# Modulation products spread over four column strips of the array, and the residual gate's weights used in fp32 as they are loaded

## The chip, the cores and the metric

The kernel is one program on one core of a Trainium2 chip. Its metric is the device time of a run in microseconds (us). TensorE (PE in the rows; PEld is its weight load) multiplies, VectorE (DVE), ScalarE (ACT) and GpSimd (POOL) do the elementwise work, and the DMA queues that SyncE (SP) and ScalarE issue move data between HBM and the on-chip memories SBUF (inputs of the engines) and PSUM (results of TensorE).

## The reference, cut to what matters

One inference step of a decoder layer with 1024 prompt tokens and 8 decode rows (1032 columns in all), model width 2048, followed by a final norm:

```
mod = silu(c) @ w_ada + b_ada        # c: 9 rows (1 prompt, 8 decode), w_ada: 2048 x 6144
sh, sc, gt = the three thirds of mod
h  = rmsnorm(x) * (1 + sc) + sh
P  = h @ w_in                        # one combined projection
o_s5, o_rw = the two branches, from P
mixed = sigmoid(g_s5) * (o_s5 @ w_out[:1024]) + sigmoid(g_rw) * (o_rw @ w_out[1024:])
x  = x + gt * mixed;   y = rmsnorm(x) * final_g
```

The change concerns only `mod`: its first two thirds (shift and scale), which are needed before `h` and so before everything else, and its last third (the residual gate `gt`), which is needed in the last stage. All tensors are fp32.

## The kernel before

The large products (h @ w_in, the gated linear unit, w_out) run in fp16 halves: weights and data are scaled by a power of two, split into a high and a low half, and three products (high-high, high-low, low-high) are summed. One job is one tile of 128 output channels: 16 row tiles x 3 products x 3 groups of 344 to 347 columns, 144 products of line 436. `weights` prepares the next job's weights beside the running one: `wload` (L354) loads 1 MB on SP's queue into two buffers, `wscale` takes the largest magnitude (DVE L157, then a reduction over partitions on POOL, L154) and `wsplit` makes the halves (ACT L386, DVE L387).

Everything else is written as generators that yield (DVE ns, PE ns, gap ns) per step. The `Driver` books these: each call of `slot` adds the booked PE time to a counter, and a background step is put into the program once the counter has passed its due time (the counter at its last step plus its gap) and the booked DVE time is not more than 0.8 us ahead. `drain` puts in all that is left. This order of the program is only a priority: the planner that lays the instructions on each engine takes, by its own cost model, the first in this order that is ready, so work that stands later can still come earlier on an idle engine. Once laid out, each engine keeps its order and waits.

**Start.** `startup` takes the shift and the scale columns in eight blocks of 512 columns (`mod_block`), scale and shift in turn. A block loads eight slabs of w_ada of 512 KB (L218, SP's queue, four buffers `wa`), and multiplies each in fp32: the 9 columns of silu(c) are the stationary operand and 512 columns of w_ada stream, 16 products in one accumulation on partitions 0 to 8 (L223; each fp32 product shows as two records). Then ACT copies the row out (L225), four transposes put channels on partitions (L229), and DVE adds the biases. In the first four blocks each second slab is followed by a tile of x (`xload`, 516 KB). Beside the blocks run `stats` (sums of squares, the inverse root, x times it: L269 to L284) and `modulate` (L294 to L298), which needs both. The halves of h (L340, L341) come after the last block, and then the first large product.

**Residual gate.** `gt_mod` runs from the end of the recurrence on, beside the gated linear unit and the output jobs. Per tile n of 128 channels it loads 1 MB of w_ada on ACT's queue (L1370, two buffers), no sooner than output job n-2 has begun (`GQ`), takes the largest magnitude of four quarters (DVE L157, POOL L154), splits each into halves (ACT L1393, DVE L1394), and multiplies 32 times with the halves as stationary operand and 18 or 9 streaming columns (L1399, L1400); two DVE steps rescale and add the bias (L1403, L1404). Output job n needs tile n (`need`), and its `final_tiles` scales the loaded gates by it (L1500).

Of the kernel before, what the change touches and what calls it, by code (L numbers as in the profile page):

```python
# [66 lines left out]
class Driver:  # L67
    """Paces background generators against the stream of large products.

    Each generator yields (vector_ns, tensor_ns, gap_ns) per step, or None while  # L70
    something it needs has not been emitted yet.
    """
# [58 lines left out]
class Hybrid:  # L131
# [10 lines left out]
    # ---------------------------------------------------------------- helpers  # L142
    def pow2(self, am, out, n=1):
        """out[:,0,:] = 2^14 / 2^floor(log2 am), out[:,1,:] its inverse, on every partition."""
# [14 lines left out]
    def rsqrt(self, v, y, t):  # L159
        """y = v^-1/2 by ln, exp and one Newton step; t is scratch, v is left as it is."""  # L160
# [7 lines left out]
    def vexp(self, x, k, r, ki):  # L168
        """x = exp(x) on VectorE for small tiles."""
# [15 lines left out]
    # ---------------------------------------------------------------- constants  # L185
# [24 lines left out]
    # ---------------------------------------------------------------- modulation  # L210
    def mod_block(self, col, stage, row, out, xload=None):
        """out(i, psum[128, 9]) for the four 128-channel tiles of modulation columns col..col+511."""
# [3 lines left out]
        for j in range(8):  # L216
            wa = stage(j)
            nc.sync.dma_start(wa, d["w_ada"][256 * j:256 * j + 256, col:col + 512].rearrange("(k p) n -> p k n", p=128))  # L218
            if xload is not None and j % 2:
                xload()  # L220
            for i in range(2):
                kt = 2 * j + i
                nc.tensor.matmul(q[0:9, :], self.csil[:, kt, :], wa[:, i, :], start=(kt == 0), stop=(kt == 15))  # L223
            yield (0, 1716, 0)
        nc.scalar.copy(row, q[0:9, :])  # L225
        yield (0, 0, RGAP)
        q2 = self.ps.tile([128, 4, 16], F32, name="pmt", tag="up")
        for i in range(4):
            nc.tensor.transpose(q2[:, i, 0:9], row[:, 128 * i:128 * i + 128], self.c["ident"][0:9, 0:9])  # L229
        out(q2)  # L230
        yield (300, 1704, 0)

    def startup(self, st, jobs):
        """h = rmsnorm(x) (1 + scale) + shift, as halves under one power of two.

        That power comes from a bound: a normalised row has no element above sqrt(DM).
        """
# [12 lines left out]
        mrow = xp.tile([9, 512], F32, name="mrow")  # L250
# [3 lines left out]
        nc.scalar.activation(out=self.csil, in_=self.csil, func=AF.Silu)  # L254
        H, HL, A = self.H, self.HL, self.As
# [92 lines left out]
    # ---------------------------------------------------------------- large products  # L348
# [8 lines left out]
    def wscale(self, job):  # L357
        """The power of two of a product's weights."""
# [16 lines left out]
    def wsplit(self, job):  # L375
        """Halves of a product's weights."""
# [15 lines left out]
    def weights(self, nxt, after):  # L392
        """Beside a product: the halves of the next one's weights, then the scale of those after them."""
# [14 lines left out]
    def run_jobs(self, jobs):  # L408
        """Runs the products in order; the weights of the next one are split while one runs."""
# [37 lines left out]
    def product_by_rows(self, job):  # L447
        """The first product takes the rows of h as they come."""
# [11 lines left out]
    # ---------------------------------------------------------------- projections  # L460
# [11 lines left out]
    def job_rw(self, idx, dst, flag, need=None, post=None):  # L472
        """A token-shifted tile: dst[:, 0:1032] = p (1 - mu) + p_prev mu."""
# [85 lines left out]
    def job_gate(self, which, n, dst=None):  # L559
        """sigmoid of a gate tile, to scratch in DRAM or to a tile on chip."""  # L560
# [15 lines left out]
    # ---------------------------------------------------------------- RWKV-7  # L576
# [37 lines left out]
    def rw_prep(self):  # L614
        """First half of each pair's preparation: everything that needs no buffer of the running recurrence."""
# [64 lines left out]
    def bdq(self, k):  # L680
        """Block diagonal form of the operands of chunks 2k, 2k+1."""
# [53 lines left out]
    def rw_side(self):  # L735
        """Token-major operands of the recurrence and the bonus term, beside the inversion."""
# [96 lines left out]
    def rw_tail(self):  # L833
        """Group norm, bonus and gate of a pair, beside the operands of the next."""
# [41 lines left out]
    def rw_sample(self):  # L876
        """Operands of the decode rows, with (head parity, pair, row) on partitions."""
# [18 lines left out]
    def sample(self):  # L896
        """One step of the recurrence for the decode rows, where the S5 operand of the outputs will lie."""
# [73 lines left out]
    # ---------------------------------------------------------------- S5  # L971
# [24 lines left out]
    def s5_system(self, st):  # L996
        """Tiles of the discretised system, made beside the modulation."""
# [13 lines left out]
    def il(self, b, g):  # L1011
        """Transposed input operand of group g of block b: it lies where the states of block b + 1 will."""
# [5 lines left out]
    def s5_pre(self):  # L1018
        """Discretised system and its powers; every value lies in both halves of the partitions."""
# [82 lines left out]
    def s5_powers(self, b, name, e1, e2, nt, op):  # L1102
        """[128, 8, nt, 16]: powers of the system on two stacked operands of a block of eight groups."""
# [14 lines left out]
    def s5_outer(self, b):  # L1118
        """Output powers of a block."""
# [5 lines left out]
    def s5_prep(self, b):  # L1125
        """Transposed input powers of a block and the kernel of its chunks."""
# [66 lines left out]
    def s5_runs(self, q):  # L1193
        """States within runs of eight chunks, for a quarter of the groups."""
# [18 lines left out]
    def s5_fix(self, b):  # L1213
        """States before the runs, carried into the chunks of the runs, for a block."""
# [129 lines left out]
    def gt_mod(self, st):  # L1344
# [30 lines left out]
        for n in range(16):  # L1375
# [5 lines left out]
            for q in range(4):  # L1381
                self.absmax(am[:, q:q + 1], w[q], axis=XY)
                yield (600, 0, 0)
# [413 lines left out]
```

## Time and profile before

| what | us |
|---|---|
| median of the 3 runs shown | 3095.9 |
| the runs | 3097.41, 3074.23, 3095.9 |
| span of the profiled execution | 3069.5 |
| TensorE busy in that span | 2792.1 (91%) |
| VectorE busy in that span | 2108.3 (69%) |

The profiled execution's own time is not listed beside its span; the lowest of the three runs lies 4.7 us above the span, the median 26.4 us. In the page's strip of 40 slices of 76.7 us the DMA engines are over 90% busy in the first slice alone, and TensorE is at nine tenths or more in 25 of the 40. The chain of work that ended last is 40% TensorE, 31% VectorE and 16% DMA. All times below are us from the start of the span unless ns is written.

### The profile page before, as it was taken

What the parts mean: (1) busy time and instruction counts of PE and PEld (TensorE: products, weight loads), DVE (VectorE), ACT (ScalarE), POOL (GpSimd) and SP (SyncE); (2) the same over time, 40 slices, a digit from 0 to 9 for tenths busy, and PEclk for the clock granted to TensorE, in tenths of its full rate; (3) what the DMA queues carried; (4) which work ended last, traced back from release to release, by engine and by line L of the source; (5) the groups of instructions that cost most, each with busy time, mean ns of one, the idle gap of its engine ahead of it and who ended that gap; (6) DMA issues with size and microseconds to landing.
All of it is one profiled execution on the core that took longest, in us unless ns stands there. A gap on an engine that the chain in (4) does not pass through costs nothing.

```text
span 3069.5 us, 47775 instructions
## 1 busy us (share of the span) xinstructions
PE 2792.1 (91%) x18266; PEld 1826.5 (60%) x18266; DVE 2108.3 (69%) x5152; ACT 1023.5 (33%) x1783; POOL 472.9 (15%) x764
## 2 busy tenths in 40 slices
PE   7889999999989999899998998999998978888987
PEld 1156666666656666576675665665765645555655
DVE  5589688745675857767668658677675595767765
ACT  2143223425243143242332432432421223433431
POOL 1201000011111111021121110210211122111213
PEclk9999999999999999999999999999999988999999
DMA  9724443331222223213231232132233344843443
GB/s 318 270 63 98 78 92 86 84 95 50 61 66 60 62 55 81 68 45 76 55 81 52 59 80 56 57 75 58 55 82 80 115 154 128 274 121 110 142 124 125
DMA packets 434165, 298.39 MB, mean 97 GB/s; under 512 B 115120, under 2 KB 400464, under 8 KB 432656
## 3 DMA queue, kind: packets, MB, share of 16 engines
q1 hardware_dynamic: 397648, 277.71, 33.1%
q10 hardware_dynamic: 36128, 17.33, 2.0%
q8 instruction: 144, 2.36, 0.3%
q14 instruction: 85, 0.70, 0.1%
q0 software_dynamic: 160, 0.30, 0.0%
HBM read 241.93 MB, written 53.35 MB: 96 GB/s over the span
## 4 chain that ended last, share of the span: by engine, by line
PE 40%; DVE 31%; DMA 16%; issue 6%; ACT 4%; POOL 2%; SPq 1%; ACTq 0%; POOLq 0%; DVEq 0%
PE pg L436 27%; DMA ws<-w_in 5%; DVE TM L781 5%; DMA od<-BV 4%; DVE ZB L783 4%; DVE wlo L387 3%; DVE wam L157 3%; PE pmod L223 2%; DMA ws<-w_out 2%; PE pma L720 2%; PE up L823 1%; PE sp L822 1%; PE up L817 1%; ACT whi L386 1%; DVE OLo L1432 1%
## 5 line engine op out<-in xcount | busy, mean ns | idle before, releaser
L436 PEld LDWEIGHTS <-whi 128*128 128x128 f16 x9600 | 944.8, 99 | 576.7 <-issue 99.8
L436 PE MATMUL pg<-H,whi 128*128 128x344 f16 (+2 forms) x3840 | 1200.7, 313 | 68.6 <-DVE ZB L500 39.1
L436 PE MATMUL pg<-H,wlo 128*128 128x344 f16 (+2 forms) x3840 | 1200.3, 313 | 1.4 <-DVE wlo L387 1.4
L436 PE MATMUL pg<-HL,whi 128*128 128x344 f16 (+2 forms) x3840 | 1200.4, 313 | 0.0
L436 PEld LDWEIGHTS <-wlo 128*128 128x128 f16 x4800 | 475.6, 99 | 256.6 <-issue 17.8
L386 ACT ACTIVATE whi<-ws,wsc 128x512 f16<-128x512 f32 x404 | 265.7, 712 | 489.5 <-DVE wsc L150 315.0
L157 DVE TENSOR_REDUCE wam<-ws 128x1 f32<-128x512 f32 x404 | 266.6, 679 | 137.8 <-DMA ws<-w_in 106.0
L387 DVE SCALAR_TENSOR_TENSOR wlo<-ws,wsc,whi 128x512 f16<-128x512 f32 x404 | 304.3, 780 | 59.3 <-ACT whi L386 58.2
L436 PE MATMUL pg<-OH,whi 128*128 128x344 f16 (+3 forms) x960 | 308.1, 321 | 22.7 <-ACT whi L386 14.9
L436 PE MATMUL pg<-OH,wlo 128*128 128x344 f16 (+3 forms) x960 | 308.0, 321 | 7.8 <-DVE wlo L387 7.8
L436 PE MATMUL pg<-OLo,whi 128*128 128x344 f16 (+3 forms) x960 | 308.3, 321 | 5.0 <-DVE OLo L1432 5.0
L781 DVE TENSOR_TENSOR TM<-ZB 128x252 f32<-128x252 f32 (+52 forms) x504 | 178.7, 355 | 89.1 <-DMA ZB<-c_t 78.6
L783 DVE TENSOR_TENSOR ZB<-ZB,TM 128x252 f32<-128x252 f32 (+52 forms) x504 | 179.8, 357 | 10.5
L154 POOL PARTITION_ALL_REDUCE wg<-wm x105 | 50.6, 482 | 862.0 <-DVE wm L157 452.9
L814 POOL TENSOR_SCALAR SG<-S,GC 128x128 f32<-128x128 f32 x120 | 98.7, 823 | 360.1 <-DVE S L825 224.5
L812 ACT COPY XR<-xp 64x128 f32<-64x128 f32 x128 | 33.0, 258 | 350.2 <-DVE XS L811 334.3
L223 PE MATMUL pmod<-wa,csil 128*9 128x512 f32 x256 | 118.6, 616 | 17.4 <-DMA wa<-w_ada 17.4
L825 DVE SCALAR_TENSOR_TENSOR S<-sp,GC,SG 128x128 f32<-128x128 f32 x120 | 41.6, 347 | 73.0 <-POOL SG L814 37.4
L684 ACT COPY BT<-ZB 64x128 f32<-64x128 f32 x256 | 75.3, 296 | 32.4 <-PE pma L720 23.0
L223 PEld LDWEIGHTS pmod<-wa,csil 128*9 128x9 f32 x256 | 22.3, 93 | 106.1 <-issue 67.0
L817 PE MATMUL up<-XS,TT 128*128 128x128 f32 x256 | 56.7, 304 | 28.1 <-DMA TT<-dT 14.1
L720 PE MATMUL pma<-AR,BT 128*128 128x128 f32 x512 | 71.6, 283 | 4.3 <-DVE AR L711 2.3
(459 smaller groups left out, 3373.4 us busy)
## 6 DMA issues: line engine op xcount, KB each, us to landing
ws<-w_in SPq DMA_DIRECT2D x162, 512.0 KB
wa<-w_ada SPq DMA_DIRECT2D x64, 512.0 KB
sg<-sgd SPq DMA_DIRECT2D x32, 516.0 KB
gw<-w_ada ACTq DMA_DIRECT2D x32, 512.0 KB
ws<-w_out SPq DMA_DIRECT2D x32, 512.0 KB
XT<-xT SPq DMA_DIRECT2D x16, 516.0 KB
xo<-xT SPq DMA_DIRECT2D x16, 516.0 KB
ZB<-dA SPq DMA_DIRECT2D x8, 1024.0 KB
```

What stands on the lines that cost most here:

```text
L154: self.nc.gpsimd.partition_all_reduce(out, in_, 128, bass_isa.ReduceOp.absmax)
L157: self.nc.vector.tensor_reduce(out=out, in_=in_, axis=axis, op=ALU.max, apply_absolute_value=True)
L223: nc.tensor.matmul(q[0:9, :], self.csil[:, kt, :], wa[:, i, :], start=(kt == 0), stop=(kt == 15))
L386: nc.scalar.activation(out=hi[:, ks, :], in_=s, func=AF.Copy, scale=job.sc[:, 0, 0:1])
L387: nc.vector.scalar_tensor_tensor(out=lo[:, ks, :], in0=s, scalar=job.sc[:, 0, 0:1], in1=hi[:, ks, :], op0=ALU.mult, op1=ALU.subtract)
L436: nc.tensor.matmul(q[:, :w], a[:, wk, :], b[:, rk, g0:g1], start=(n == 0), stop=(n == tot - 1))
L684: self.nc.scalar.copy(self.BT[k % 2][i][64 * h:64 * h + 64, :, 64 * h:64 * h + 64], t[64 * h:64 * h + 64, 128 * k:128 * k + 128].rearrange ...
L720: nc.tensor.matmul(q[:, e, 128 * i:128 * i + 128], w[:, e, :], self.AR[:, a, 128 * e:128 * e + 128], start=True, stop=True)
L781: nc.vector.tensor_tensor(out=TM, in0=row.unsqueeze(1).to_broadcast([128, n, m]), in1=TL[:, :n, k:k + 1].to_broadcast([128, n, m]), op=ALU ...
L783: nc.vector.tensor_tensor(out=TL[:, :n, k + 1:], in0=TL[:, :n, k + 1:], in1=TM, op=ALU.subtract)
L814: nc.gpsimd.tensor_scalar(out=self.SG, in0=S0, scalar1=g, scalar2=None, op0=ALU.mult)
L817: nc.tensor.matmul(up[:, 0, :], self.TT[:, a, :], xs, start=True, stop=True)
```

## The change

Both uses of w_ada now go through one helper, `mod_step`. Row tile kt writes its product to the 32 partitions that begin at 32 (kt mod 4), so that four accumulations stand in four column strips of the array. The stationary operand is silu(c) padded with zeros from 9 to 32 columns (`cond`), and the four partial sums are added by one more product with a 0/1 matrix `sel`, which takes the place of the transposes. The residual gate's weights are the streaming operand in fp32, 128 columns at a time; its magnitudes, powers of two, halves and rescaling are gone. The booked times and gaps of the steps change with them. The rest of the diff replaces comment lines by blank ones.

```diff
     def mod_block(self, col, stage, row, out, xload=None):
...
-            for i in range(2):
-                kt = 2 * j + i
-                nc.tensor.matmul(q[0:9, :], self.csil[:, kt, :], wa[:, i, :], start=(kt == 0), stop=(kt == 15))
-            yield (0, 1716, 0)
-        nc.scalar.copy(row, q[0:9, :])
+            self.mod_step(q, self.cs32, wa, 2 * j)
+            yield (0, 600, 0)
+        nc.scalar.copy(row, q)
         yield (0, 0, RGAP)
         q2 = self.ps.tile([128, 4, 16], F32, name="pmt", tag="up")
         for i in range(4):
-            nc.tensor.transpose(q2[:, i, 0:9], row[:, 128 * i:128 * i + 128], self.c["ident"][0:9, 0:9])
+            nc.tensor.matmul(q2[:, i, 0:9], row[:, 128 * i:128 * i + 128], self.sel, start=True, stop=True)
         out(q2)
-        yield (300, 1704, 0)
+        yield (300, 1000, 0)
+
+    def mod_step(self, q, cs, w, k0):
+        for i in range(w.shape[1]):
+            kt = k0 + i
+            s = 32 * (kt % 4)
+            self.nc.tensor.matmul(q[s:s + 32], cs[:, kt, :], w[:, i, :], start=(kt < 4), stop=(kt >= 12))
+
+    def cond(self, pool):
+        t = pool.tile([128, 16, 32], F32, name="cs32", tag="cs32", bufs=1)
+        self.nc.gpsimd.memset(t, 0.0)
+        self.nc.vector.tensor_copy(t[:, :, 0:9], self.csil)
+        self.sel = pool.tile([128, 9], F32, name="sel", tag="sel", bufs=1)
+        w = self.c["ident"].rearrange("p (g x) -> p x g", g=4)[:, 0:9]
+        self.nc.vector.tensor_reduce(out=self.sel, in_=w, axis=AX, op=ALU.add)
+        return t
...
     def startup(self, st, jobs):
-        mrow = xp.tile([9, 512], F32, name="mrow")
+        mrow = t("mrow", 512)
...
+        self.cs32 = self.cond(xp)
...
     def gt_mod(self, st):
-        m, g, cs = small("gcm", 1), small("gcg", 1), small("gcs", 2, 1)
...
+        cs32 = self.cond(pool)
+        yield (300, 0, 2000)
...
             w = load(n)
             yield (0, 0, 6000)
-            am = small("gam", 4, bufs=2)
-            for q in range(4):
-                self.absmax(am[:, q:q + 1], w[q], axis=XY)
-                yield (600, 0, 0)
...
-            self.gmax(g, m1)
-            yield (100, 0, 2500)
-            self.pow2(g, sc)
...
-            for q in range(4):
-                ks = slice(4 * q, 4 * q + 4)
-                nc.scalar.activation(out=hi[:, ks], in_=w[q], func=AF.Copy, scale=sc[:, 0, 0:1])
-                V.scalar_tensor_tensor(out=lo[:, ks], in0=w[q], scalar=sc[:, 0, 0:1], in1=hi[:, ks], op0=ALU.mult, op1=ALU.subtract)
-                yield (700, 0, 0)
-            yield (0, 0, GGAP)
-            q = self.ps.tile([128, 18], F32, name="pmg", tag=("xp", "sp")[n % 2])
-            for k in range(16):
-                nc.tensor.matmul(q, hi[:, k, :], C[:, k, :], start=(k == 0), stop=False)
-                nc.tensor.matmul(q[:, 0:9], lo[:, k, :], C[:, k, 0:9], start=False, stop=(k == 15))
-            yield (0, 1000, 0)
-            gt = self.gt[:, n, :]
-            V.tensor_scalar(out=gt, in0=q[:, 0:9], scalar1=iv, scalar2=c["b_ada"][:, 32 + n:33 + n], op0=ALU.mult, op1=ALU.add)
-            V.scalar_tensor_tensor(out=gt, in0=q[:, 9:18], scalar=iv, in1=gt, op0=ALU.mult, op1=ALU.add)
-            yield (200, 0, 0)
+            q = self.ps.tile([128, 128], F32, name="pmg", tag=("xp", "sp")[n % 2])
+            for h in range(2):
+                self.mod_step(q, cs32, w[h], 8 * h)
+            row = small("grow", 128)
+            nc.scalar.copy(row, q)
+            yield (0, 1300, 1500)
+            q2 = self.ps.tile([128, 16], F32, name="pmh", tag="up")
+            nc.tensor.matmul(q2[:, 0:9], row, self.sel, start=True, stop=True)
+            V.tensor_scalar(out=self.gt[:, n, :], in0=q2[:, 0:9], scalar1=c["b_ada"][:, 32 + n:33 + n], scalar2=None, op0=ALU.add)
+            yield (200, 250, 0)
             self.flags.add(f"gt{n}")
```

## Rows read from the trace of the kernel before

**Rows 1.** The page, part 1: busy us, share of the span, instructions.
```profile
PE 2792.1 (91%) x18266; PEld 1826.5 (60%) x18266; DVE 2108.3 (69%) x5152; ACT 1023.5 (33%) x1783; POOL 472.9 (15%) x764
```
**Rows 2.** DMA totals of 0:150; windows: PE, PEld, DVE, ACT, POOL busy, clock, DMA share, GB/s.
```profile
DMA packets 29243, 45.02 MB, mean 300 GB/s; under 512 B 6018, under 2 KB 10677, under 8 KB 29237
20.00:25.00 5.00, 4.63 (x12) 0.83 (x10) 4.77 (x25) 1.72 (x3) 0.00 (x0) 1.00 1.10 358
50.00:55.00 5.00, 3.76 (x9) 0.91 (x10) 3.71 (x4) 3.31 (x4) 3.03 (x2) 0.66 0.51 193
125.00:130.00 5.00, 5.00 (x13) 1.03 (x12) 5.00 (x6) 0.00 (x0) 4.92 (x2) 1.00 0.87 304
```
**Rows 3.** Chain of waits in the startup: start us, us, what.
```profile
87.52 13.83 PE pmod L223 x32
...
134.33 12.99 PE pmod L223 x30
...
157.29 16.63 DVE HL L341 x14
```
**Rows 4.** PE waits in 2475:3050: us in total, times, longest.
```profile
PE pmg L1399 <- ACT gw L1393: 25.6, 13, 6.0
PE pg L436 <- ACT whi L386: 18.4, 5, 7.4
PE pmg L1400 <- DVE gw L1394: 11.7, 30, 0.8
```
**Rows 5.** ACT timeline: the gate's splits of tiles 3 and 15: start us, us.
```profile
2704.56 2.54 ACT L1393 ACTIVATE gw<-gw,gsc 128x512 f16<-128x512 f32 x4
...
3001.95 2.56 ACT L1393 ACTIVATE gw<-gw,gsc 128x512 f16<-128x512 f32 x4 [4.17 <-DVE oinv L1511]
```
**Rows 6.** Chain of waits, a long undisturbed stretch of large products.
```profile
320.28 42.44 PE pg L436 x291
```
**Rows 7.** PE timeline around the gate's products of tile 10: start us, us, [idle before].
```profile
2874.39 0.18 PE L1399 MATMUL pmg<-csil,gw 128*128 128x18 f16 x1 [2.38 <-ACT gw L1393]
...
2880.57 0.49 PE L436 MATMUL pg<-OLo,whi 128*128 128x344 f16 x1
2881.36 0.31 PE L436 MATMUL pg<-OLo,whi 128*128 128x344 f16 x1
```
**Rows 8.** PE timeline: fp32 products that all stand in the first 16 columns.
```profile
188.03 1.91 PE L1159 MATMUL pmx<-CB,D 128*16 128x128 f32 x16
```
**Rows 9.** PE timeline: fp32 products that alternate between two 64x64 tiles.
```profile
2316.24 0.92 PE L885 MATMUL pms<-c_mat,SMP 64*64 64x64 f32 x24
```
**Rows 10.** Line 1565: weight loads of wide fp32 stationary tiles, ns min/median/max.
```profile
L1565 PEld LDWEIGHTS pst<-ones,ACC x18: 171/178/318, 3026.5 to 3055.5; 128*110 128x110 f32 x8, 128*120 128x120 f32 x6, 128*116 128x116 f32 x4
```
**Rows 11.** Tile gw: the gate's work on DVE and ACT, ns min/median/max.
```profile
L157 DVE TENSOR_REDUCE gam<-gw x64: 668/676/687, 2486.3 to 2988.3; 128x1 f32<-128x512 f32 x64
L1393 ACT ACTIVATE gw<-gw,gsc x64: 704/706/722, 2537.5 to 3003.8; 128x512 f16<-128x512 f32 x64
L1394 DVE SCALAR_TENSOR_TENSOR gw<-gw,gsc,gw x64: 743/746/753, 2538.4 to 3004.7; 128x512 f16<-128x512 f32 x64
```
**Rows 12.** Windows of the gated linear unit's stage, columns as in rows 2.
```profile
2475.00:2600.00 125.00, 90.47 (x582) 54.72 (x580) 90.69 (x192) 38.31 (x65) 29.05 (x29) 0.86 0.43 131
```
**Rows 13.** DVE timeline of the startup: the root's start, the scaling of x, its modulation.
```profile
102.16 1.10 DVE L278 TENSOR_SCALAR HL<-pst 128x344 f32<-128x344 f32 x2 [11.88 <-PE pst L277]
...
114.28 13.81 DVE L284 TENSOR_TENSOR XT<-XT,RS 128x1032 f32<-128x1032 f32 x12
...
132.69 8.76 DVE L298 TENSOR_SCALAR XT<-XT,GS,SH 128x1024 f32<-128x1024 f32 x12
```
**Rows 14.** A gate tile's loads: issue on ACT's queue, then the DVE step on its second half.
```profile
2635.12 1.86 ACTq L1370 DMA_DIRECT2D gw<-w_ada  x2
...
2647.43 1.28 DVE L157 TENSOR_REDUCE gam<-gw 128x1 f32<-128x512 f32 x2 [4.86 <-DMA gw<-w_ada]
```
**Rows 15.** Line 223: weight loads and products, ns min/median/max.
```profile
L223 PEld LDWEIGHTS pmod<-wa,csil x256: 86/91/141, 7.9 to 146.3; 128*9 128x9 f32 x128
```

More of the change, by code (lines that the diff above doesn't have):

```diff
@@ L1347, in gt_mod @@
         V = nc.vector
-        XY = mybir.AxisListType.XY
         pool = self.pool("gtp", stack=st)
@@ L1352, in gt_mod @@
             yield None
-        m, g, cs = small("gcm", 1), small("gcg", 1), small("gcs", 2, 1)
-        self.absmax(m, self.csil, axis=XY)
-        self.gmax(g, m)
-        yield (200, 0, 2000)
-        self.pow2(g, cs)
-        t = self.ot.tile([128, 448], F32, name="gct", tag="glv")[:, 0:144].rearrange("p (k b) -> p k b", b=9)
-        V.tensor_copy(t, self.csil)
-        C = self.csil.bitcast(F16)
-        nc.scalar.activation(out=C[:, :, 0:9], in_=t, func=AF.Copy, scale=cs[:, 0, 0:1])
-        V.scalar_tensor_tensor(out=C[:, :, 9:18], in0=t, scalar=cs[:, 0, 0:1], in1=C[:, :, 0:9], op0=ALU.mult, op1=ALU.subtract)
-        yield (800, 0, 0)
-        hi, lo = (small(f"gw{i}", 16, 128, dt=F16) for i in range(2))
+        cs32 = self.cond(pool)
+        yield (300, 0, 2000)
         def load(n):
@@ L1371, in load @@
                                     .rearrange("(k p) n -> p k n", p=128))
-                w += [t[:, 0:4, :], t[:, 4:8, :]]
+                w.append(t)
             return w
@@ L1379, in gt_mod @@
             yield (0, 0, 6000)
-            am = small("gam", 4, bufs=2)
-            for q in range(4):
-                self.absmax(am[:, q:q + 1], w[q], axis=XY)
-                yield (600, 0, 0)
-            m1, g, sc, iv = small("gm1", 1, bufs=2), small("gg", 1, bufs=2), small("gsc", 2, 1, bufs=2), small("giv", 1, bufs=2)
-            self.absmax(m1, am)
-            self.gmax(g, m1)
-            yield (100, 0, 2500)
-            self.pow2(g, sc)
-            V.tensor_tensor(out=iv, in0=sc[:, 1, :], in1=cs[:, 1, :], op=ALU.mult)
-            yield (400, 0, 300)
-            for q in range(4):
-                ks = slice(4 * q, 4 * q + 4)
-                nc.scalar.activation(out=hi[:, ks], in_=w[q], func=AF.Copy, scale=sc[:, 0, 0:1])
-                V.scalar_tensor_tensor(out=lo[:, ks], in0=w[q], scalar=sc[:, 0, 0:1], in1=hi[:, ks], op0=ALU.mult, op1=ALU.subtract)
-                yield (700, 0, 0)
-            yield (0, 0, GGAP)
-            q = self.ps.tile([128, 18], F32, name="pmg", tag=("xp", "sp")[n % 2])
-            for k in range(16):
-                nc.tensor.matmul(q, hi[:, k, :], C[:, k, :], start=(k == 0), stop=False)
-                nc.tensor.matmul(q[:, 0:9], lo[:, k, :], C[:, k, 0:9], start=False, stop=(k == 15))
-            yield (0, 1000, 0)
-            gt = self.gt[:, n, :]
-            V.tensor_scalar(out=gt, in0=q[:, 0:9], scalar1=iv, scalar2=c["b_ada"][:, 32 + n:33 + n], op0=ALU.mult, op1=ALU.add)
-            V.scalar_tensor_tensor(out=gt, in0=q[:, 9:18], scalar=iv, in1=gt, op0=ALU.mult, op1=ALU.add)
-            yield (200, 0, 0)
+            q = self.ps.tile([128, 128], F32, name="pmg", tag=("xp", "sp")[n % 2])
[8 more added lines that the diff above has]
+            yield (200, 250, 0)
             self.flags.add(f"gt{n}")
```

## The prediction

> **What bounds the kernel now.** I read the page's busy times first, then the windows and the chain of waits of the two stretches where w_ada is used. TensorE is busy 91% of the span [rows 1], so time can be won only where it waits, or where it does products that get shorter. The change touches two such places.
>
> In the startup, 45.0 MB are moved in the first 150 us [rows 2]. Early, where x is loaded too, the DMA engines are full and deliver 358 GB/s; later they deliver 304 at a share of 0.87, and TensorE is busy without a break [rows 2]. The chain says the same: a block of 32 records is one unbroken 13.83 us, 0.432 each, and the last one ends at 147.3 [rows 3]. So the first half hangs on DMA, the second on TensorE. The window at 50 shows a block's end in the DMA-bound half: 193 GB/s, since the four buffers stay full until TensorE goes on [rows 2]. After 147.3 come the scale, the low halves of h from 157.3 on [rows 3], and the first large product.
>
> In the last stage, TensorE waited 25.6 us for the high halves of the gate's weights, 11.7 for the low ones, and 18.4 for those of the large products [rows 4]. The splits of gate tiles 3 and 15 are 297.4 us apart [rows 5]: 24.8 us for each of 12 output jobs. A record of 344 columns takes 42.44 / 291 = 0.1458 [rows 6], so the 144 records of a job need 21.0 of the 24.8; the other 3.8 are the gate's products and the waits. How one such event looks: TensorE idles 2.38 before the gate's first product, and six us later the large products still take 0.49; only from 2881.4 on do they take 0.31 again [rows 7]. So a pause has a second price: after a like one in the startup the mean granted clock is 0.66, a stretch at the lower of the two levels [rows 2].
>
> **The change part by part.** *Products in strips, price of one.* fp32 products that share one strip of the array took 1.91 / 16 = 0.119 per record of 128 columns [rows 8]. The only products before that alternate between parts of the array took 0.92 / 24 = 0.038 per record of 64 columns [rows 9], where the unshared rate would give 0.060: a factor of 1.56, entry and exit included. They differ in rows and columns of the array, those of the change in columns alone, so this is the nearest row and not the same case. Bounds: no sharing (factor 1) and four strips at once (factor 4). I take 1.56, because a product's two records go to the same strip one behind the other there as here.
>
> *Startup.* With 1.56 a block needs 13.83 / 1.56 = 8.9 us of TensorE, and its 4.2 MB need 11.7 at 358 GB/s: DMA becomes the limit. All 45.0 MB at 358 are 125.8, and the first few us bring little, so the last block would end near 129 instead of 147.3: 18 less. The four wide products with the 0/1 matrix have two weight loads of 0.178 each [rows 10], 4 x 0.36 = 1.4 behind the last block, at most that much more; and one stall like that at 50 costs about another. I take 16 less, bounds 0 (TensorE goes on setting the pace) and 21. The padding and the 0/1 matrix are three small steps on POOL and DVE, beside the first slabs' transfer; without that cover under 1 us.
>
> *Gate, what goes.* Per tile DVE loses four maxima of 0.676 and four low halves of 0.746, 5.7 us, and ACT four of 0.706, 2.8 us [rows 11]; a reduction on POOL and some small steps go as well. What is late next at this place is the DMA of the slab, and then TensorE itself. What comes: a row copy on ACT and one bias step on DVE, both shorter than one of the steps removed, and the next tile's DMA issues stand behind the copy on ACT.
>
> *Gate, TensorE.* 16 products are 32 records: 32 x 0.119 = 3.8 unshared, 3.8 / 1.56 = 2.45 shared, plus 0.36 for the two loads of the summing product [rows 10]: 2.8. A job is then 21.0 + 2.8 = 23.8, against 24.8 now, if nothing is waited for: 1.0 x 12 jobs = 12. Bounds: 21.0 + 3.8 + 0.4 = 25.2 (0.4 x 12 = 5 worse) and 21.0 + 1.0 + 0.4 = 22.4 (29 better). The large products' own halves come sooner by the 5.7 us of DVE that are gone from between them, so they do not set the pace. This is the point of the sum: the fp16 products were cheap, the change buys freedom from waits with longer products, and most of the 37 us of waits is paid back.
> By the Trainium skill, "TensorE: Matmul & The Clock Gate", Part 3 (Measured speedup vs the span model), three column strips give 2.38; by that figure a tile would be 3.8 / 2.38 = 1.6, a job 23.0, and these 12 jobs 22 better instead of 12. No run here shows it yet, and the sum does not use it.
>
> *Before these jobs.* In the gated linear unit's stage DVE is busy 90.7 of 125 us and TensorE hardly more, 90.5 [rows 12]. Tiles 0 and 1 lose 11.4 us of DVE there; about half of it I count as on the path: 6. Tiles 2 and 3, in the first output jobs, at 1.0 each: 2. Bounds 0 and 13.
>
> *Sum.* 16 + 12 + 6 + 2 = 36 less. Against the profiled span of 3069.5 this gives 3033; against the median of 3095.9, which lies 26 above that span, 3060. I forecast against the median, and keep for the low end that one of the three runs was 22 below it.
>
> **The rivals.**
> *Strips share fully (0.20).* Factor 4. Startup 21, a job 22.4 for 12 jobs 29, the rest 9: 59 less, 3037. For it speaks that four accumulations on separate partitions are independent; against it, that the alternating pair of rows 9 did not reach 2.
>
> *Strips do not share (0.11).* The change does not do what it says: all use the same 128 rows, and the records run one behind the other. Startup 0, jobs 5 worse, 8 from DVE's relief: 3 less, 3093, no change. The row that speaks against it is rows 9, which has two tiles; none has column strips alone.
>
> *The normalisation of x falls behind the last block (0.13).* A block now books 8 x 0.6 + 1.0 = 5.8 us instead of 8 x 1.716 + 1.704 = 15.4, eight of them 46 instead of 123. The 16 squares are spaced 2.5 us of booked time, 40 in all, and so the scaling of x comes after the blocks in the program's order. If the planner does not draw it forward, three parts stand behind the last block: 12.1 for the root (102.2 to 114.3), 18.4 for the scaling (16 of 13.81 / 12) and 8.8 for the twelve tiles of the modulation that were done before [rows 13], 39 in all; 36 - 39 = 3 more than before, 3099. Against it: the order is only a priority, and DVE waited 11.88 for TensorE before the root alone [rows 13], time in which such work fits.
>
> *TensorE waits for the gate's DMA (0.09, the slow side).* Before, DVE took the wait for the slab; now the products follow the load directly, 6.0 us of booked time behind it, in TensorE's own queue, with the large products behind them. The issue at 2635.1 had its second half in use at 2647.4, 12.3 later [rows 14]. If each of 14 tiles is late by 12.3 - 6.0 = 6.3, that is 88, less the 36: 52 more, 3148. It decides from a mean wait of 36 / 14 = 2.6 us on. Against it: the planner sees the load too and places the products where it believes them ready, and that load ran beside others at the stage's start.
>
> *The weight loads come into the open (0.05, slow as well).* In the startup a load of 0.091 [rows 15] lay hidden in the 0.432 between two records of one strip. If switching strips puts each load between two products, it costs 32 x 0.091 = 2.9 per tile, 46 for 16 tiles, and 256 x 0.091 = 23 in the startup; with no sharing otherwise (3 less) that is 66 more, 3162.
> The Trainium skill states a rule that points there ("TensorE: Matmul & The Clock Gate", Part 3, The mechanism): a load overlaps with running products only if it goes to other rows of the array. The rows of line 223 disagree for one strip; none shows several.
>
> **How the numbers follow.** The forecast (0.42) is 3060, its own range 3048 to 3076 from the terms' bounds. A measurement of this kernel can tell about 1%, 31 us, from no change. Of the forecast 0.30 lies beyond that and 0.12 within; the full sharing adds 0.20 to faster; no sharing and the late normalisation add 0.24 to no change; the two slow ones make 0.14. So faster 0.50, same 0.36, slower 0.14. The range goes from 3015 (full sharing, and a run 22 below the median) to 3100 (late normalisation); the two slow cases are left out.
>
> **What would show it.** Startup: the last block's end near 131, records of line 223's successor that overlap, DMA near 358 GB/s after 90 us. Sharing: the 32 records of a gate tile in about 2.5 us. Gate: no wait of TensorE on ACT or DVE halves; no wait of over 2 us on the slab; gate tiles about 24 us apart. Late normalisation: the scaling of x (L284 before) starting behind the last block. The forecast is wrong if the strips run one behind the other, if TensorE's waits on the slab sum to more than 30 us, or if the stretch from the last block to the halves of h grows beyond the 10 us it has now.

## The result, and the profile after

The changed kernel took 3039.7 us, median of 4 runs (3025.6 to 3043.0), beside 3086.6 for the kernel before on the same chip: ratio 0.9841 [0.9809, 0.9873]. That is 47 us less by these medians, 49 (39 to 59) by the ratio, by which all kernels are compared below. The forecast was 3060, 36 less. Both profiled executions are single ones: 3069.5 us of span before, shorter than the shortest run shown of that kernel, and 3041.2 after, which belongs to the longest of the four runs. So the two spans lie closer together than the medians.

The page after, part 1, answers to [rows 1]:

```profile
PE 2743.5 (90%) x18330; PEld 1819.4 (60%) x18330; DVE 2028.4 (67%) x4892; ACT 984.4 (32%) x1734; POOL 461.2 (15%) x749
```

TensorE is as full as before; 49 of its busy microseconds are gone.

**Do the strips share?** The timeline of TensorE of the kernel after, around one gate tile and, further down, another with its summing product; it answers to [rows 7] (columns as there):

```profile
2730.40 0.31 PE L453 MATMUL pg<-OH,whi 128*128 128x344 f16 x1
2730.64 1.08 PE L236 MATMUL pmg<-gw,cs 128*32 128x128 f32 x32
2731.66 0.32 PE L453 MATMUL pg<-OLo,whi 128*128 128x344 f16 x1
...
2870.36 1.08 PE L236 MATMUL pmg<-gw,cs 128*32 128x128 f32 x32
...
2874.68 0.39 PE L1393 MATMUL pmh<-sel,grow 128*128 128x9 f32 x2 [0.79 <-ACT grow L1390]
```

32 records in 1.08 us, 0.034 each, against 0.119 in one strip [rows 8]: a factor of 3.5, where the prediction took 1.56. The first tile again, in two windows so short that they catch its first four and its first eight records alone:

```profile
2730.64 0.32 PE L236 MATMUL pmg<-gw,cs 128*32 128x128 f32 x4
2730.64 0.43 PE L236 MATMUL pmg<-gw,cs 128*32 128x128 f32 x8
```

A single record lasts 0.27 to 0.30, so the first four stand in the array together, and the next four follow 0.11 later, which is the distance of two records in one strip. No idle time stands before the tile, and the large products go on at 0.31 to 0.32 behind it. Still, entry and exit have a price: from the last large product before the tile to the first behind it, 2730.40 to 2731.66, it is 1.26 us; without the usual 0.15 between two large products, and without eight rounds of 0.11, some 0.2 are left for each tile.

**The startup.** Windows of the kernel after, columns as in [rows 2]:

```profile
20.00:25.00 5.00, 3.89 (x10) 0.37 (x8) 4.92 (x39) 1.52 (x4) 0.00 (x0) 0.50 1.10 363
50.00:55.00 5.00, 5.00 (x24) 2.24 (x24) 3.98 (x3) 2.17 (x3) 3.75 (x2) 0.50 0.19 60
90.00:95.00 5.00, 3.95 (x18) 0.60 (x16) 0.86 (x2) 3.40 (x3) 0.00 (x0) 0.68 0.33 93
125.00:130.00 5.00, 2.72 (x20) 1.27 (x20) 3.70 (x7) 0.59 (x1) 0.00 (x0) 1.00 0.95 356
```

At 125 TensorE is now half idle (2.72 of 5 us) and DMA nearly full, as predicted. But twice the transfers fall off, to 60 and 93 GB/s. The first stop, on TensorE's and then on ScalarE's timeline (start us, us, what, [idle before]):

```profile
49.86 1.88 PE L227 MATMUL pmt<-sel,mrow 128*128 128x9 f32 x8 [5.25 <-ACT mrow L223]
```

```profile
44.87 2.56 ACT L403 ACTIVATE whi<-ws,wsc 128x512 f16<-128x512 f32 x4 [11.77 <-DVE wsc L150]
47.34 2.00 ACT L286 ACTIVATE HL<-XT 128x1032 f32<-128x1032 f32 x2
49.24 0.56 ACT L223 COPY mrow<-pmod 128x512 f32<-128x512 f32 x1
```

The copy of the block's row stands on ScalarE behind four halves of another product's weights and two squares; TensorE waits 5.25 us for it and frees none of the four buffers, so the transfers have nowhere to go. The chain of waits at the startup's end, which answers to [rows 3]:

```profile
132.78 6.03 DMA wa<-w_ada
138.85 1.08 PE pmod L236 x4
140.01 0.59 ACT mrow L223
...
148.23 0.41 POOL gmx L154
...
150.91 1.29 DVE HL L358
```

The products of the last block end at 139.9 instead of 147.3, the low halves of h begin 6.4 us earlier, at 150.9.

**The gate.** TensorE's waits in 2475:3050 of the kernel after, which answer to [rows 4]:

```profile
PE pmt L967 <- DVE smq L963: 18.7, 1, 18.7
PE pmh L1393 <- ACT grow L1390: 18.3, 13, 4.7
PE pg L453 <- ACT whi L403: 10.2, 1, 10.2
```

The 37 us of waits for the gate's halves are gone; 18.3 for the row copy took their place. There is no wait for the gate's slab. The 18.7 of the first line stands in the gated linear unit's stage and is taken up again further down. One window from the first output of the gated linear unit to the last output evacuation, of the kernel before and of the one after:

```profile
2493.20:3052.50 559.30, 487.05 (x3494) 313.55 (x3492) 388.73 (x888) 196.38 (x303) 111.15 (x152) 0.93 0.46 140
```

```profile
2494.80:3024.00 529.20, 469.93 (x3536) 309.50 (x3534) 307.44 (x628) 156.93 (x254) 106.75 (x136) 0.95 0.48 148
```

30.1 us shorter: TensorE is busy 17.1 less and idle 13.0 less, VectorE loses 81 of 389. I call this window the gate's stretch below. The stretch between startup and gate, in which nothing was changed, took 2335.9 before and 2343.9 after, and 2327.5 to 2351.1 over all kernels here; so what two single profiles say of a whole span is uncertain by a dozen microseconds, and the ratios carry the verdicts.

### The profile page after: what moved, and what is told of

Read it like the earlier page. It is cut to its first block, busy times and chain, and to the rows that moved or that the text cites. A ratio compares the mean times of both kernels' runs of the same rounds, so it can differ in the third digit from the quotient of the medians.

```text
span 3041.2 us, 47546 instructions
## 1 busy us (share of the span) xinstructions
PE 2743.5 (90%) x18330; PEld 1819.4 (60%) x18330; DVE 2028.4 (67%) x4892; ACT 984.4 (32%) x1734; POOL 461.2 (15%) x749
## 4 chain that ended last, share of the span: by engine, by line
PE 40%; DVE 28%; DMA 19%; ACT 4%; issue 4%; POOL 2%; SPq 1%; ACTq 0%; POOLq 0%; DVEq 0%
PE pg L453 28%; DMA ws<-w_in 7%; DVE TM L798 4%; DVE ZB L800 4%; DMA od<-BV 4%; DVE wlo L404 3%; DVE wam L157 3%; DMA wa<-w_ada 3%; DMA sg<-sgd 2%; PE pma L737 2%; PE up L840 1%; ACT whi L403 1%; PE sp L839 1%; PE up L834 1%; PE pmod L236 1%
## 5 line engine op out<-in xcount | busy, mean ns | idle before, releaser
L453 PE MATMUL pg<-OH,whi 128*128 128x344 f16 (+3 forms) x960 | 301.0, 314 | 22.0 <-ACT whi L403 10.2
L453 PE MATMUL pg<-OLo,whi 128*128 128x344 f16 (+3 forms) x960 | 301.1, 314 | 3.2 <-DVE OLo L1422 3.2
L453 PE MATMUL pg<-OH,wlo 128*128 128x344 f16 (+3 forms) x960 | 300.9, 313 | 1.0 <-DVE wlo L404 1.0
L236 PE MATMUL pmod<-wa,cs 128*32 128x512 f32 x256 | 76.7, 866 | 39.1 <-DMA wa<-w_ada 27.6
L1505 DVE SCALAR_TENSOR_TENSOR sg<-pg,oinv,sg 128x344 f32<-128x344 f32 (+3 forms) x96 | 54.8, 571 | 47.6 <-PE pg L453 47.5
L147 DVE TENSOR_SCALAR p2m<-wg 128x1 f32<-128x1 f32 x105 | 15.9, 151 | 102.0 <-POOL wg L154 101.1
```

What stands on the lines that cost most here:

```text
L236: self.nc.tensor.matmul(q[s:s + 32], cs[:, kt, :], w[:, i, :], start=(kt < 4), stop=(kt >= 12))
L453: nc.tensor.matmul(q[:, :w], a[:, wk, :], b[:, rk, g0:g1], start=(n == 0), stop=(n == tot - 1))
L1505: V.scalar_tensor_tensor(out=f, in0=q[:, :g1 - g0], scalar=job.inv[:, w:w + 1], in1=f, op0=ALU.mult, op1=ALU.mult)
```

## Experiments

**Which part gives how much?** Each part alone. The kernel with the new startup alone is the changed kernel with the whole `gt_mod` of the kernel before; the kernel with the new gate alone is the changed kernel with `mod_block` and the 9-row `mrow` of the kernel before, and without the padding step in the startup.

> Strips in the startup alone; the residual gate by fp16 halves as before. Theory A (nearly all of the gain lies in the last stage; the startup ends 6 us sooner in the trace and gives part of that back later): 0 to 10 us faster than before, ratio 0.997 to 1.000. Rival B (the prediction's sum, 16 of 36 us from the startup): 16 us faster, ratio 0.995. Both: the low halves of h begin near 151 instead of 157.

> The new residual gate alone; the startup as before. Theory A: 30 to 45 us faster than before, ratio 0.985 to 0.990, the stretch of the 16 output jobs near 372 us instead of 404. Rival B: 20 us faster, ratio 0.9935.

Startup alone: 0.9967 [0.9950, 0.9983], 10 us less (5 to 15), the first low half at 148.9. Gate alone: 0.9852 [0.9823, 0.9880], 46 less (37 to 55), its stretch 523.4. So the gate carries the gain, twice what the prediction gave it (12 + 6 + 2), and the startup falls short of its 16.

**Is it the strips?** Both parts with all products in one strip, so that the summing product reads the 32 rows of that strip alone:

```diff
-            s = 32 * (kt % 4)
-            self.nc.tensor.matmul(q[s:s + 32], cs[:, kt, :], w[:, i, :], start=(kt < 4), stop=(kt >= 12))
+            self.nc.tensor.matmul(q[0:32], cs[:, kt, :], w[:, i, :], start=(kt == 0), stop=(kt == 15))
```

> The changed kernel with all 16 products of an accumulation in the first strip (partitions 0 to 31), in both places; the summing product takes that strip alone. Theory A (four strips run fully side by side, 1.08 us for a gate tile): a gate tile's 32 records take 3.6 to 3.8 us, 2.6 more for each of 16 tiles, and the startup goes back by 6: 45 us slower than the changed kernel, near the kernel before, ratio 0.997 to 1.003. Rival C (the strips matter little, the gain is that nothing is split any more and DVE and ACT are relieved): within 10 us of the changed kernel, ratio 0.984 to 0.988.

1.0099 [1.0074, 1.0125], 31 us slower than before. Half a gate tile on TensorE's timeline, the gate's stretch, and VectorE's timeline in the startup:

```profile
2700.78 1.93 PE L235 MATMUL pmg<-gw,cs 128*32 128x128 f32 x16 [2.02 <-DMA gw<-w_ada]
```

```profile
2533.50:3096.40 562.90, 514.32 (x3529) 352.05 (x3526) 311.20 (x628) 156.81 (x254) 108.07 (x136) 0.96 0.45 139
```

```profile
167.76 18.38 DVE L300 TENSOR_TENSOR XT<-XT,RS 128x1032 f32<-128x1032 f32 x16
```

16 records take 1.93, 0.121 each, as one strip did before [rows 8]. The stretch is back at 562.9 (559.3 before), with VectorE as empty as after the change (311 us busy against 307): without sharing TensorE's longer products, 514 us busy against 470, eat all of it. The startup shows something else: the scaling of x runs only at 167.8, behind the last block, and the first low half stands at 197.6, 40 later than before. That is the rival of the late normalisation, in a kernel whose booked times are those of the change. Not all of the 40 is its price: the products of the last block end later here too, at 154.1 (chain of waits) instead of 147.3.

```profile
141.11 12.99 PE pmod L235 x30
```

From there to the first low half it is 43.5 us instead of 10.0, so 33.5 more, where the rival had 39. In TensorE's order the products that sum the squares now stand behind the products of all eight blocks; in the changed kernel they stand behind those of four and a quarter. What made the planner order them so is not settled here. This run's total is thus no measure of sharing alone; its gate's stretch is.

**What holds the startup?** Six buffers for the slabs, in the changed kernel and in the kernel before:

```diff
-        wap = self.pool("wap", bufs=4, stack=st)
+        wap = self.pool("wap", bufs=6, stack=st)
```

> The changed kernel with six buffers for the startup's slabs of w_ada instead of four. Theory D (the startup falls short of the DMA rate because the four buffers fill whenever TensorE stands at a block's end, twice for 7 to 10 us): 3 to 8 us faster than the changed kernel, the last block ends near 133 instead of 141, no window below 200 GB/s before 130 us. Rival E (the DMA engines give no more in the later blocks, whatever the depth): last block's end within 2 us of 141, no change of the time.

> The kernel before with six buffers for w_ada's slabs instead of four, nothing else. Theory A (in the startup of the kernel before, TensorE at 13.8 us a block is the limit from the middle on, so deeper buffers have little to win; it takes strips and depth together): the scale of h (first low half, 157.3 before) at 153 to 158, ratio to the kernel before 0.998 to 1.002. Theory B (the depth of the buffers alone gives what the changed kernel with six buffers won over four): the first low half at 140 to 146, ratio 0.993 to 0.996.

The changed kernel comes to 0.9780 [0.9755, 0.9805], 68 us less than before and some 20 less than with four buffers; I had expected 3 to 8. The first low half is at 138.0; in the six kernels with the new startup in strips and four buffers it lies between 148.6 and 153.0. A window of the changed kernel with four buffers, and the same with six:

```profile
100.00:130.00 30.00, 20.68 (x98) 5.41 (x96) 27.67 (x32) 1.76 (x3) 5.92 (x6) 0.94 0.89 308
```

```profile
100.00:130.00 30.00, 21.16 (x102) 5.40 (x101) 25.54 (x34) 1.76 (x3) 7.46 (x8) 1.00 1.00 346
```

TensorE's waits for the row copy are the same (10.7 and 10.4 us in 0:200), but now the transfers go on through them. The kernel before gains nothing from six buffers (1.0000 [0.9983, 1.0017], first low half 158.2), as theory A said, but not wholly for its reason. Its chain of waits, and POOL's timeline:

```profile
127.31 12.99 PE pmod L223 x30
```

```profile
141.41 0.41 POOL L154 PARTITION_ALL_REDUCE wg<-wm  x1 [6.09 <-issue]
149.08 0.24 POOL L295 TENSOR_TENSOR XT<-XT,SH 128x32 f32<-128x32 f32 x1 [7.26 <-issue]
155.70 0.41 POOL L154 PARTITION_ALL_REDUCE gmx<-am  x1 [6.38 <-issue]
```

The products of its last block end at 140.3, 7 us earlier than before, although a block still takes TensorE as long; but a reduction of weights had slipped in front of the last step on POOL, and three gaps of 6 to 7 us there used those 7 up.

**Could the row copy go to another engine?** On top of six buffers, with the longer gap of the last experiment below:

```diff
-        nc.scalar.copy(row, q)
-        yield (0, 0, RGAP)
+        nc.vector.tensor_copy(row, q)
+        yield (600, 0, RGAP)
```

> As the kernel with six buffers and the longer gap, and the startup's row copy on VectorE instead of ScalarE (where it stood behind the halves of the weights). Theory A (TensorE's 10 us of waits for row copies still set the startup's end): first low half at 130 to 134 instead of 138, ratio 0.001 to 0.002 below that kernel. Theory B (with six buffers the transfers go on through these stops, and 45 MB at some 376 GB/s are the limit): first low half at 137 to 139 and the same ratio. Theory C (VectorE, full from 100 to 120 us, makes TensorE wait longer): 140 to 145, ratio 0.001 to 0.003 above.

0.9818 [0.9792, 0.9844], slower by 23 us than the kernel with the copy on ScalarE (0.9744); the first low half is at 143.5. Theory C, and more than its size. TensorE's waits in 0:200:

```profile
PE pmt L227 <- DVE mrow L223: 18.8, 8, 6.7
```

18.8 instead of 9.9: the copy at 109.2, for one, stands behind ten scalings of x. Where the rest of the loss lies, the profiles do not tell: their spans differ by only 10, since the one of the faster kernel belongs to its longest run (3014.5) and the one of this kernel to its shortest (3024.6).

**Is the gate's gain the relief of VectorE and ScalarE?** The removed maxima and halves put back as dead work, nothing using them, first on the slab, then on a tile that lies ready:

```diff
...
+            for k in range(4):
+                s = w[k // 2][:, 4 * (k % 2):4 * (k % 2) + 4, :]
+                self.absmax(am[:, k:k + 1], s, axis=mybir.AxisListType.XY)
+                yield (600, 0, 0)
+            for k in range(4):
...
+                nc.scalar.activation(out=hi, in_=s, func=AF.Copy, scale=1.0)
+                V.scalar_tensor_tensor(out=lo, in0=s, scalar=1.0, in1=hi, op0=ALU.mult, op1=ALU.subtract)
+                yield (700, 0, 0)
```

That is the edit on the slab; on the ready tile `s` is `cs32`, the padded silu(c).

> The changed kernel, with the work that was taken off VectorE and ScalarE put back as work that nobody uses: per gate tile four maxima of a quarter and four splits of a quarter into halves, after the tile is done. Theory A (the gain is that TensorE no longer waits for the halves): at most 10 us slower than the changed kernel, ratio to before 0.984 to 0.988. Rival C (the gain is the relief of VectorE, 5.7 us per tile, and ScalarE, 2.8): most of the 32 us of the output jobs comes back, ratio 0.993 to 0.996.

> The changed kernel with the removed work of VectorE and ScalarE put back as dead work of the same shapes, now on the padded silu(c) that lies ready, so that VectorE does not wait for the gate's slab (with the slab itself as operand it waited 40 us for its transfer, 9 in the kernel before). Nothing uses its results. Theory A (the work itself brings back what that kernel lost): ratio 0.992 to 0.995 to the kernel before, some 20 us or more above the changed kernel. Theory B (the loss was VectorE's wait for the slab's transfer with other work queued behind it): ratio 0.984 to 0.988, within 10 us of the changed kernel.

On the slab: 0.9934 [0.9918, 0.9951], so 29 of the 49 us come back that the change had won. VectorE's waits in the output jobs, of this kernel and of the kernel before:

```profile
DVE gam L157 <- DMA gw<-w_ada: 40.2, 14, 9.0
```

```profile
DVE gam L157 <- DMA gw<-w_ada: 9.4, 6, 4.9
```

It is not a clean copy of the old load: VectorE waits 40 us for the slab, with its other work queued behind. On a ready tile, without that wait: 0.9891 [0.9855, 0.9928], 15 back, between the two theories. Its gate's stretch:

```profile
2477.10:3022.40 545.30, 475.99 (x3553) 312.24 (x3551) 370.57 (x749) 188.13 (x310) 110.67 (x136) 0.94 0.47 144
```

545.3 against 529.2, with VectorE at 371 (before: 389). So about a third of the gain is the work itself, but loosely measured: 4 to 27 us by the ends of the interval, the changed kernel's ratio taken as exact. The rest is something that this run does not put back; what is left to name, without a run that shows it, is that the products no longer stand at the end of a line of maxima, a reduction on POOL, a scale and halves. To put back POOL's reduction alone, or the line with dead products, was not tried.

**Could the kernel before simply have started its products later?** Its gap from halves to products doubled:

```diff
-GGAP = 4000
+GGAP = 8000
```

> The kernel before, with the gap ahead of the gate's fp16 products doubled from 4 to 8 us of booked time, so that they stand later in TensorE's order. Theory A: TensorE's waits for the halves (37.3 us) fall by more than half, 15 to 25 us faster than before, ratio 0.992 to 0.995. Rival C (VectorE's load sets the pace of a job): the waits move to the weights of the large products, no change, ratio 0.998 to 1.002.

1.0002 [0.9984, 1.0019]: nothing. Counted in the two traces, 15 of the 16 tiles' products now stand behind 20 to 191 more of the large products than before. TensorE's waits for the halves in this kernel:

```profile
PE pmg L1399 <- ACT gw L1393: 27.8, 12, 5.2
...
PE pmg L1400 <- DVE gw L1394: 6.4, 14, 1.6
```

27.8 for the high halves, as before (25.6), and 6.4 for the low ones (11.7): the products moved, and most of the wait moved with them, so the halves came later too. Theory A fails; that VectorE's load sets the pace, as rival C has it, is not shown by this run alone.

**Is what is left in a job TensorE's?** The gate's products done twice:

```diff
-            for h in range(2):
+            for h in (0, 1, 0, 1):
```

> The changed kernel with each gate tile's 16 products done twice. Theory A (the output jobs are now bound by TensorE): 14 to 16 tiles x 1.1 us, 15 to 18 us slower than the changed kernel, ratio 0.989 to 0.991. Rival F (the jobs are still bound by the chain that loads and splits the next weights, TensorE has room): under 5 us slower, ratio 0.984 to 0.986.

0.9871 [0.9845, 0.9897], about 9 us above the changed kernel (1 to 17 by the ends of the interval), for 16 x 1.08 = 17 us more of products; the gate's stretch is 534.6, 5.4 longer. TensorE's wait for the row copy in the output jobs fell from 16.4 to 6.4, which is where most of the rest went. So a microsecond of TensorE in a gate tile seems to cost about half of one; the interval leaves room for nearly nothing and for all of it.

**Can the wait for the row copy be planned away?** 4.5 instead of 1.5 us booked before the summing product, in the changed kernel and in the one with six buffers:

```diff
-            yield (0, 1300, 1500)
+            yield (0, 1300, 4500)
```

> The changed kernel with the gap ahead of the summing product raised from 1.5 to 4.5 us of booked time, so that ScalarE's row copy is done when TensorE comes to it. Theory A: the 16 to 18 us of waits on the row copy fall below 5, and 10 to 15 us go with the lower clock after such waits: 8 to 15 us faster than the changed kernel, ratio 0.979 to 0.982. Rival G (the wait fills room that TensorE has anyway): no change, 0.984.

> The changed kernel with six buffers for w_ada's slabs and with 4.5 instead of 1.5 us of booked time between the row copy and the summing product of the gate. Theory A (the two places are far apart in the program, so their gains add): about 20 and 5 us below the changed kernel, ratio 0.975 to 0.978 to the kernel before; TensorE's wait for the row copy of the gate 9 us or less in sum, and the first low half of h near 138. Theory B (the gap only moves waits): ratio 0.978 to 0.981, as with six buffers alone, with other waits of the same sum in place of those for the row copy.

Alone 0.9825 [0.9802, 0.9848], 5 us better than the change, within its interval. With six buffers 0.9744 [0.9714, 0.9774], 3003.6 us: the fastest kernel here, 79 us (70 to 88) below the one before. TensorE's waits from 2475 on in it:

```profile
PE pmt L967 <- DVE smq L963: 17.6, 1, 17.6
PE pg L453 <- ACT whi L403: 11.0, 2, 10.5
PE pmh L1393 <- ACT grow L1390: 8.8, 3, 3.8
```

The wait for the row copy is halved and none grew in its place; the gate's stretch is 516.1, and 516.4 with four buffers, against 524.7 and 529.2 without the gap. Both pairs say 9 to 13 us; the ratios, whose intervals overlap, 5 and 11.

## Why the prediction was right, and where it was wrong

**The direction and its reasons hold:** the startup's second half passed from TensorE to DMA, the waits for the gate's halves went, no wait for the slab came, and the scaling of x was drawn forward. The time lies between 3015 and 3100. The likeliest case, 3060 with its own range of 3048 to 3076, fell all the same: of the mechanism's cases the full sharing came true (0.20), with less from the startup and more from the gate than it had. That its 3037 lies so near the 3039.7 measured is in part luck: it stood for 59 us less, and 47 to 49 were measured; the rest is that the median of the kernel before, 3095.9 when the forecast was made, is 3086.6 with a fourth run.

**The price of one product in strips was the term mis-sized.** The step said 1.56 from [rows 9], and 2.45 us for a tile; it took 1.08. Two errors lie in it. The first is how the row was read: I divided a whole event by its records, and the last record's own length is in it. With the length of a single record (views of lines 885 and 1159 of the kernel before, and of the gate's tile after; ns min/median/max):

```profile
L885 PE MATMUL pms<-c_mat,SMP x24: 218/218/267, 2316.2 to 2316.9; 64*64 64x64 f32 x24
...
L1159 PE MATMUL pmx<-CB,D x128: 269/273/421, 188.0 to 283.8; 128*16 128x128 f32 x128
```

```profile
L236 PEld LDWEIGHTS pmg<-gw,cs x512: 106/110/110, 2496.2 to 2964.3; 128*32 128x32 f32 x171
L236 PE MATMUL pmg<-gw,cs x512: 272/273/297, 2496.2 to 2964.4; 128*32 128x128 f32 x171
```

One strip goes at (1.91 - 0.27) / 15 = 0.109 a record, the alternating pair at (0.92 - 0.22) / 23 = 0.030 for 64 columns where 0.109 / 2 = 0.055 would be unshared: 1.8 of 2. Read so, the row of before says that sharing is nearly full. The second error is larger: that row has two tiles, the change has four strips, and the sum took the factor of two for four. Its reason, that a product's two records go to the same strip one behind the other, does not slow them here: four records in a row start together. The tile's 32 records are eight rounds of four, and (1.08 - 0.27) / 7 gives 0.116 a round, against 0.109 for one record in one strip: a factor of 3.8 of 4. The full-sharing rival, which the same rows, read for four strips, would have made the forecast, gave the gate 29 + 9 = 38; its stretch became 30 shorter in the change and 36 with the gate alone, the ratio of that run says 46.
By the Trainium skill ("TensorE: Matmul & The Clock Gate", Part 3, Measured speedup vs the span model), three column strips give 2.38. No run here has three; the trace's 3.5 for four, last record included, neither bears that figure out nor goes against it.

**The startup was over-sized:** 16 expected, 10 measured alone (5 to 15). The step that failed is 45.0 MB at 358 GB/s. Four buffers hold 2.1 MB, some 6 us of transfer, and two stops of TensorE, one of which the prediction did count, left none free. With six buffers 45.1 MB came within 138 us, the products of the last block ended at 126.9 (129 in the prediction), and the first low half came 19 earlier than before: the 16 were there, behind too few buffers. Two smaller readings of this part failed as well. The padding of silu(c) was to hide behind the first transfers; in this trace its copy stands on VectorE behind a step that waits for another transfer, and TensorE begins at 11.4 instead of 8.0. No price of it shows: two other kernels with this startup begin at 11.6 and 11.8 and have their first low half at 149.6 and 148.6, and one that begins at 8.0 has it at 153.0. And a slab holds two products, so where TensorE waits for each slab, two strips work and not four: a slab's four records take 1.05 us there (115.24 of the kernel after, at the upper clock), against some 1.5 for its 512 KB at 358 GB/s. What this costs at the lower clock is not shown.

**The gated linear unit's stage gave none of its 6.** Its start and the first output evacuation lay 155.6 us apart before and 156.9 after. TensorE's timeline after:

```profile
2532.58 0.48 PE L967 MATMUL pmt<-c_mat,smq 64*64 64x64 f32 x4 [18.75 <-DVE smq L963]
2543.30 0.47 PE L453 MATMUL pg<-OH,whi 128*128 128x344 f16 x1 [10.24 <-ACT whi L403]
```

VectorE has less to do there, but TensorE now waits 18.75 us for a step of the state's last part on VectorE, and 10.24 for weights, waits of a size that [rows 4] did not have. The longer one goes with the new gate: 17.6 to 19.7 in the seven kernels that have it in strips and no work put back, 10.1 and 4.0 in the two with dead work, 5.4 in one strip, under 2 in the four kernels with the old gate. On its way stands POOL, where a reduction of weights comes ahead of the state's own step:

```profile
2521.19 0.41 POOL L154 PARTITION_ALL_REDUCE wg<-wm  x1 [5.98 <-DVE ZG L1472]
2529.06 0.59 POOL L960 TENSOR_TENSOR gvr<-gvr,c_mhalf 128x1 f32<-128x1 f32 x1 [7.46 <-DMA ZG<-zsd]
```

VectorE's step waits for the second of them. What brought this order about, and what the stage would take without the wait, was not tried.

**"They do not set the pace"** was said of the large products' halves once VectorE is relieved, and held: of 18.4 us in five waits 10.2 in one is left, in the gated linear unit's stage and none in the output jobs. But the sum gave VectorE's relief no price of its own in those jobs, and the dead work says 15 us (4 to 27).

**The rivals.** No sharing: it does not happen, but the kernel in one strip shows its price: 3.6 us more of the gate's stretch than before, where 5 more in the jobs and 8 less from VectorE's relief were worked out. Late normalisation: it does not happen in the change, and costs 33.5 behind the last block in the kernel where it does (39 worked out). Waits for the gate's DMA: none in the change. Exposed loads: the loads of the 32 records, 0.110 each, make 3.5 us and lie within 1.08, so they run beside the products and beside each other.
The rule of the Trainium skill that a load overlaps only with products in other rows of the array ("TensorE: Matmul & The Clock Gate", Part 3, The mechanism) is not borne out: all loads here go to the same 128 rows.

## What to carry to other kernels

To read a rate off a pipelined engine, take the last instruction's own length out of the event first: (event - one) / (count - 1), and where several run side by side, count the rounds and not the instructions. And do not carry a factor measured on two parts over to four. When an engine is relieved in a stage that transfers feed, price the depth of their buffers with it: here two more buffers moved the startup's end by 13 us, twice what the change itself did. And a step taken off a chain of engines is worth more or less than its busy time: put back as dead work, this one returned 15 of 49 us, 4 to 27 by its interval.

## What the runs showed of the hardware that I had not expected

Four fp32 products with 32 output rows each, on four column strips, start a round of four records of 128 columns some 0.11 us after the last, the distance of single records in one strip. Where fp16 products of the full array stand on both sides, some 0.2 us a tile is lost, without an idle time that the profile shows.

In parts of the startup TensorE's granted clock now was the lower of its two levels, 0.50 or 1.2 GHz (mean of 0:150: 0.74), and that did not hold up the transfers there: 363 GB/s in 20:25, against 358 at full clock before [rows 2]. TensorE's idle share alone does not tell where: in 20:25 it was busy 3.89 of 5 us at 0.50, in 125:130 only 2.72, at 1.00.

A reduction over partitions on POOL that follows an element-wise step there starts some 6 us behind it in the startup, with nothing that the profile shows in between. POOL's timeline of the kernel before, and of the kernel in one strip, where the last step before the reduction was another reduction:

```profile
148.81 0.25 POOL L295 TENSOR_TENSOR XT<-XT,SH 128x32 f32<-128x32 f32 x1 [6.70 <-DVE SH L313]
154.84 0.41 POOL L154 PARTITION_ALL_REDUCE gmx<-am  x1 [5.78 <-issue]
```

```profile
134.15 0.41 POOL L154 PARTITION_ALL_REDUCE wg<-wm  x1 [41.43 <-DVE wm L157]
158.62 0.35 POOL L154 PARTITION_ALL_REDUCE gmx<-am  x1 [24.06 <-DVE am L348]
```

In the kernel before, VectorE's last step for `am`, which the reduction reads, ended at 150.6, 4.2 us ahead of it; in the kernel in one strip it ended 0.1 ahead. So some 4 us of this gap stand on the path to the halves of h, and as much in the changed kernel (143.9 to 148.2). What fills the gap is not shown. To move the element-wise step off POOL was not tried.
